# PSUM banks named by the kernel, and two kinds of loads issued by GpSimd

## The chip, the cores and the metric

The program runs on one core of one Trainium2 chip. A core has TensorE (PE; PEld is its weight load), VectorE (DVE), ScalarE (ACT) and GpSimd (POOL), and SyncE (SP), whose work here is to issue DMAs. TensorE writes its results to PSUM, which has eight banks of 128 partitions by 2 KB; a tile of this kernel's P() fills one bank. The metric is the device time of one execution in microseconds (us).

## The reference, cut to what matters

One layer of a diffusion backbone, float32, width 1024, 512 latent tokens and 256 context tokens:

1. h = modulated layer norm of the tokens; z = h @ w_in.
2. Branch A, RWKV-7 in 16 heads of 64 and both directions: each of k, r, v is a part of z with a three-tap shift along the tokens. A decay d and a gate a come from two small products after tanh. Per token, S = S diag(d) - (S kk)(kk a)^T + v k^T, and y = S r. The scan runs over the context first and then over the latent tokens.
3. Branch B, spatial gating; both branches are gated and projected, and added to x with a layer norm.
4. A mixture of 16 experts that choose their tokens (router, top-k, three products per expert), and the last layer norm.

## The kernel before, in words

The work falls into stages. From 0 to 305 us a loop over `ct` (eight blocks of 128 channels) makes k, r and v by zmm(), which takes one PSUM tile `zl` for the latent tokens and one `zc` for the context. shift_in() then makes the three taps: a ScalarE copy (L352) and two VectorE steps (L354, L356) that read the PSUM tiles; `kt`, `rt` and `vt` name the results for k, r and v. prep_a() multiplies the small products (PSUM tiles `b1` and `b2`, shown as `b` in the profile), prep_tanh() reads them on ScalarE (L427, L428), z_sq() follows (L402), then prep_scan() (L436 to L445, with `Ge` at L443). prep_v() transposes v (PSUM tiles `vT`, read by ScalarE at L514). One round of the loop issues, in this order: z_k(ct, 0), prep_d1(ct - 1), z_k(ct, 1), prep_v(ct - 1), prep_bonus(ct - 1), prep_a(ct, 0), prep_tanh, z_sq, prep_scan, prep_kd, z_r, prep_k, more VectorE steps, z_v, prep_a(ct, 1), prep_tanh. The loop stands in a manual schedule: each engine runs its instructions in this written order.

From 305 to 575 us TensorE makes the gating parts of z. From 575 to 862 us the scan runs, in 12 steps of 64 tokens (four of context, eight latent) and two directions. Its order is written out in a list of short words, PLAN and PLAN_END. In a word such as `s3.1` the letter is the part, then come the step and the direction: z (zed), q (query), y (you), s (state), w (why) are the products that follow one another; K is keys_t (the transposes `bk` of `xx`, L856); l loads `al` and `xx` (prep_load, with GpSimd's memsets of `al`), a makes the pairwise products (PSUM tile `sc`, VectorE L695); v loads `Dt` and starts a wave, 31 small VectorE steps (L717, L719), run by the words p; F and D end a wave; o writes to `Asd`, from which `Dt` is read (L723), i reads `x` from Xpd and `tp` from Xsd. S, U and R are loads: sv_load, uv_load and ro_load. uv_load fills one half of a tile, and in you() ScalarE writes the other half (L877, L878); state() reads both (PSUM tile `sp`, added to `sv` by VectorE, L894). Inside PLAN each engine keeps the written order; in PLAN_END and elsewhere outside a manual schedule SP, TensorE and ScalarE do, and a planner orders VectorE and GpSimd.

From 862 to 1024 us come the readout, the branches, the output projection and the router; then to the end the experts, for which 376 MB of weights and more are streamed in.

All PSUM tiles come from P(), L70. Before, it names one tag for all of them, with eight buffers: the bank of a new tile is the one that the planner's own times say is freed first. On the chip a new tile's first write waits until every reader of that bank's last tile is done.

Of the kernel before, what the change touches and what calls it, by code (L numbers as in the profile page):

```python
# [1 line left out]

# [5 lines left out]
F32 = mybir.dt.float32  # L8
# [35 lines left out]
def block_kernel(es: ExitStack, tc, x, ctx, cT, ada_w, ada_b, pc, rows, w_ch, w_vs, w2, a2, g2, sgu_w,  # L44
                 wba, wbb, w_out, rw, e1, e3, e2, out):
    nc = tc.nc
    V, S, G, PE, SY = nc.vector, nc.scalar, nc.gpsimd, nc.tensor, nc.sync
# [6 lines left out]
    pp = es.enter_context(tc.tile_pool(name="ps", bufs=8, space=PSUM))  # L54
# [5 lines left out]
    def nm(p):  # L60
        cnt[0] += 1
        return f"{p}{cnt[0]}"

    def T(shape, name="t", dt=F32):
        return big.tile(shape, dt, name=nm(name), tag="big", bufs=NBIG)

    def K(shape, name="t", dt=F32):
        return keep.tile(shape, dt, name=nm(name), tag="keep", bufs=NKEEP)

    def P(name="p"):  # L70
        return pp.tile([128, 512], F32, name=nm(name), tag="ps")

    def mm(o, l, r, start=True, stop=True):
        PE.matmul(o, l, r, start=start, stop=stop, skip_group_check=True)  # L74
# [144 lines left out]
    def ada_chunk(ws):  # L219
        p = P("ada")  # L220
        for k in range(KT):
            g = k % 4
            mm(p[32 * g:32 * g + 32, :], sP[:, k, :], ws[k // 2][:, k % 2, :], start=(k < 4), stop=(k >= 4))
        a = T([128, 512], "adao")
        S.activation(a, p, AF.Copy)
        return a
# [9 lines left out]
    def ada_cols(n):  # L236
        a = ada_chunk(aw.pop(n))
        p = P("adt")
        for b in range(4):
            PE.transpose(p[:, b * 128:b * 128 + 128], a[:, b * 128:b * 128 + 128], ident)  # L240
        which, b0 = divmod(n * 4, 8)
        dst = md[:, which, b0:b0 + 4, :]
        V.tensor_reduce(dst, p.rearrange("p (b g m) -> p b m g", b=4, g=4)[:, :, 0:2, :], AX.X, OP.add)
        V.tensor_tensor(dst, dst, adab_col[:, which, b0:b0 + 4, None].to_broadcast([128, 4, 2]), OP.add)
        if which == 1:
            V.tensor_scalar(dst, dst, 1.0, None, op0=OP.add)
# [23 lines left out]
    for d in range(2):  # L270
        for lst, src, nme in ((w2p, w2, "w2p"), (a2p, a2, "a2p")):
            t = T([128, D], nme)
# [7 lines left out]
    def hl(k):  # L280
        return hL[0][k // 2][:, k % 2, :], hL[1][k // 2][:, k % 2, :]

    def hc(k):
        return hC[0][k // 4][:, k % 4, :], hC[1][k // 4][:, k % 4, :]
# [23 lines left out]
    for k in range(KT):  # L308
        if k % 4 == 0:
            ada_cols(k // 4)  # L310
            ada_cols(k // 4 + 2)
            if k:
                zw.step()
        for (dst, i0, n, j) in ((hl(k), 2, 4, 0), (hc(k), 0, 2, 1)):
            p = P("ht")
            w = n * 128
            for i in range(n):
                PE.transpose(p[:, i * 128:i * 128 + 128], xts[i0 + i][:, k * 128:k * 128 + 128], ident)
            t = T([128, TL], "hf")
            V.tensor_scalar(t[:, :w], p[:, :w], md[:, 1, k, j:j + 1], md[:, 0, k, j:j + 1], op0=OP.mult, op1=OP.add)  # L320
            S.activation(dst[0], t[:, :w], AF.Copy)
            G.tensor_tensor(dst[1], t[:, :w], dst[0].bitcast(F32), OP.subtract)  # L322

    def zmm(w, want_ctx):
        wh, wl = (t.rearrange("p (k n) -> p k n", k=KT) for t in w)
        pl = P("zl")
        pc_ = P("zc") if want_ctx else None
        for k in range(KT):
            st, sp = k == 0, k == KT - 1
            hh, hlo = hl(k)  # L330
            mm(pl, wh[:, k, :], hh, st, False)
            mm(pl, wh[:, k, :], hlo, False, False)
            if want_ctx:
                ch_, cl = hc(k)
                mm(pc_[:, :TC], wh[:, k, :], ch_, st, False)
                mm(pc_[:, :TC], wh[:, k, :], cl, False, False)
                mm(pc_[:, :TC], wl[:, k, :], ch_, False, sp)
            mm(pl, wl[:, k, :], hh, False, sp)
        return pl, pc_
# [31 lines left out]
    Rd_ = dp.tile([2, KT, 128, NCL, C], F32, name="Rhd")  # L371
# [262 lines left out]
    def cidx(si, d):  # L634
        lat, s = steps[si]
        n = NCL if lat else NCX
        return lat, (n - 1 - s if d else s)
# [10 lines left out]
    AL, XX, AP_, TP, X1, BK, RO, UV, SV = {}, {}, {}, {}, {}, {}, {}, {}, {}  # L648
# [7 lines left out]
    def halves(e):  # L656
        return (slice(0, 64), slice(64, 128)) if e == 0 else (slice(64, 128), slice(0, 64))
# [161 lines left out]
                r0 = e * 64  # L819
                S.activation(tp[r0:r0 + 32, d, :, 32:64], pv[r0:r0 + 32], AF.Copy)  # L820

    def vload(dst, si, d):
        lat, c = cidx(si, d)
        t0 = (TC if lat else 0) + (c ^ d) * C
        src = Vd[d][t0:t0 + C, :].rearrange("t (c e n) -> t c e n", c=KT, e=2)
        SY.dma_start(dst[64:128, 0], src[:, :, 0, :])
        SY.dma_start(dst[0:64, 1], src[:, :, 1, :])

    def sv_load(si):
        for d in range(2):  # L830
            SV[si, d] = T([128, 2, KT, C], "sv")
            vload(SV[si, d], si, d)

    def uv_load(si):
        for d in range(2):
            lat, c = cidx(si, d)
            UV[si, d] = T([128, 2, KT, C], "uv")
            vload(UV[si, d], si, d)

    def ro_load(si):  # L840
        for d in range(2):
            lat, c = cidx(si, d)
            if lat:
                ro = RO[si, d] = st_tp["ro", d, si % 2]
                for e in range(2):
                    own, oth = halves(e)
                    SY.dma_start(ro[own, e], Rd_[d, :, own, c, :].rearrange("c p n -> p c n"))

    def keys_t(si):
        for d in range(2):  # L850
# [29 lines left out]
    def state(si, d):  # L880
        bk, sv, uv, svn = BK.pop((si, d)), SV[si, d], UV[si, d], SV[si + 1, d]
        u = uidx(si, d)
        sp = P("sp").rearrange("p (c n) -> p c n", c=KT)
        idt = (si, d) in IDENT
        if idt:
# [115 lines left out]
    def finish(_):  # L1001
# [31 lines left out]
        ('b', 3): ((wave, 1),),  # L1033
        ('a', 4): ((static_pair, 0), (xx_load, 1),),
        ('a', 6): ((sv_load, 0), (uv_load, 0), (wave_in, 0), (wave_in, 1),),
        ('a', 3): ((xx_load, 0),),
    }
# [45 lines left out]
    for d in range(2):  # L1083
# [16 lines left out]
        "q10.1 p1 s9.1 U11 s9.0 w9 V10 h10.0 z10.1 X10 z10.0 p1 y10.1 h10.1 y10.0 p5 s10.1 R11 s10.0 p4 w10 p2 "  # L1100
        "i11 p1 z11.0 h10.2 p1 V11 p1 q11.1 X11 z11.1 h11.0 y11.0 q11.0 p3 y11.1 p2 h11.1 w11 h11.2 "
    ).split()
    IDENT = {(1, 0), (4, 0), (4, 1), (7, 1), (8, 0), (8, 1), (9, 1), (10, 1)}

    def finish_wave(w):
# [9 lines left out]
    def run_plan(plan, hook=None):  # L1115
        for t in plan:
            args = [int(a) for a in t[1:].split(".") if a]
            if t[0] == "h":
                hook(*args)
            elif t[0] == "t":  # L1120
                static_pair(1)
            else:
                OPS[t[0]](*args)
# [40 lines left out]
    def readout(half):  # L1164
        H = [K([128, 4, 256], "yAH", F32R) for _ in range(2)]
        L = [K([128, 4, 256], "yAL", F32R) for _ in range(2)]
        YA[half] = (H, L)
        for o, i in enumerate(HALF[half]):
            bo = GB[half][0][o]
            for b in range(2):  # L1170
                p = P("yT").rearrange("p (a n) -> p a n", a=4)
                pg = P("gg").rearrange("p (a n) -> p a n", a=4)
                t = T([128, 4, 128], "yf")
                for q in range(4):
                    ct = 4 * b + q
                    PE.transpose(p[:, q, :], yt[i][:, ct * 128:ct * 128 + 128], ident)
                    mm(pg[:, q, :], st_tp["g2"][:, ct * 128:ct * 128 + 128], sdg[:, i * 128:i * 128 + 128])
                for q in range(4):
                    ct = 4 * b + q
                    if b == 0:  # L1180
                        V.scalar_tensor_tensor(t[:, q, :], p[:, q, :], col("lnx_g", ct), bo[:, ct, :], op0=OP.mult, op1=OP.add)
                    else:
                        S.activation(t[:, q, :], p[:, q, :], AF.Copy, scale=col("lnx_g", ct))
                if b:
                    G.tensor_tensor(t, t, bo[:, 4 * b:4 * b + 4, :], OP.add)
                V.tensor_mul(t, t, pg)
                hd, ld = H[b][:, :, o * 128:o * 128 + 128], L[b][:, :, o * 128:o * 128 + 128]
                S.activation(hd, t, AF.Copy)
                V.tensor_tensor(ld, t, hd.bitcast(F32), OP.subtract)
# [169 lines left out]
    def early(si, at):  # L1359
# [8 lines left out]
        if si == nst - 1:  # L1368
# [4 lines left out]
            if at == 1:  # L1373
                readout(0)

    with tc.manual_schedule():
        run_plan(PLAN)
    run_plan(PLAN_END, early)
# [25 lines left out]
    ps = out_mm(0, (0, 1), MG.pop(0))  # L1404
# [7 lines left out]
    ps = out_mm(1, (0,), mg)  # L1412
    sid1 = out_ln(1, (0,), ps)
    next(sid1), next(sid1)
    ps = out_mm(1, (1,), mg, True)
# [28 lines left out]
    for r in range(8):  # L1444
        src = wk if r else affT
# [6 lines left out]
    p = P("sT")  # L1452
# [132 lines left out]
    e, hidT = NE - 1, hidTs.pop(NE - 1)  # L1585
# [100 lines left out]
```

## Time and profile before

| | us |
|---|---|
| runs of the kernel before | 1973.10, 1976.82, 1978.05 |
| median | 1976.82 |
| profiled execution | 1979.77 |
| its span | 1978.0 |
| TensorE busy | 1762.2 |
| VectorE busy | 919.3 |
| ScalarE busy | 604.2 |
| GpSimd busy | 239.2 |

How to read it: the profile is of one execution. A busy share over the whole span says little here, as the stages differ; the rows below give the stages apart. In a row of waits, "PE b L74 <- ACT vs L514" reads: TensorE's instruction on tile `b`, line 74, stood idle until ScalarE's instruction on `vs`, line 514, was done. A line can be that of a helper: all matmuls stand on L74, so the tile's name tells them apart. All DMAs are issued by SP; the page lists 48 of `uv<-Vd` and 32 of `ro<-Rhd`, 128 KB each.

### The profile page before, as it was taken

The numbers are of one execution on the slowest core, as the hardware profiler recorded it, in microseconds if no ns is written. First come the engines' busy times: TensorE is split into PE (matmuls) and PEld (weight loads), VectorE is DVE, ScalarE is ACT, GpSimd is POOL, SyncE is SP. The second block draws the span as 40 slices with busy tenths as digits, with TensorE's granted clock in tenths as the row PEclk, the third lists the DMA queues.
The fourth block names the chain that finished last, engine by engine and source line by source line (L and its number), as shares of the span: only waits on it lengthen the run. The fifth ranks groups of instructions, "written<-read, shape, count | busy, mean of one in ns | idle before, by whom it ended". The sixth has DMA issues, their size and how long they took to land.

```text
span 1978.0 us, 32483 instructions
## 1 busy us (share of the span) xinstructions
PE 1762.2 (89%) x13252; PEld 1122.8 (57%) x13252; DVE 919.3 (46%) x1685; ACT 604.2 (31%) x1058; POOL 239.2 (12%) x203
## 2 busy tenths in 40 slices
PE   6989999999987978788959999899998989899895
PEld 3877777878876867687844434334343323334324
DVE  6688886687837768786950020110102002020105
ACT  2666766233246645343221111101011101111101
POOL 4422234110110100055300000000000000000000
PEclk9999999999999989898969999999999999999998
DMA  9265657667697667584189999999999999999995
GB/s 331 92 194 155 188 155 238 193 225 228 237 261 160 154 146 179 114 266 138 65 348 427 426 428 426 426 427 427 426 427 427 427 427 426 427 427 427 427 418 201
DMA packets 363757, 590.34 MB, mean 298 GB/s; under 512 B 220372, under 2 KB 282324, under 8 KB 315480
## 3 DMA queue, kind: packets, MB, share of 16 engines
q1 hardware_dynamic: 363608, 588.26, 80.6%
q8 instruction: 105, 1.72, 0.3%
q14 instruction: 44, 0.36, 0.1%
HBM read 539.69 MB, written 47.71 MB: 297 GB/s over the span
## 4 chain that ended last, share of the span: by engine, by line
DMA 44%; PE 26%; DVE 11%; issue 3%; SPq 2%; ACT 1%; POOL 0%; DVEq 0%; ACTq 0%; POOLq 0%
DMA we<-in_e 42%; PE zl L74 5%; PE hh L74 3%; PE zv L74 2%; PE sc L74 2%; DVE tmpi L717 2%; PE bb L74 2%; DVE Xt L719 2%; PE yx L74 2%; PE qs L74 2%; PE yp L74 1%; PE sp L74 1%; PE zp L74 1%; PE l L74 1%; PE up L74 1%
## 5 line engine op out<-in xcount | busy, mean ns | idle before, releaser
L74 PE MATMUL hh<-we,xe 128*64 128x512 f32 x2048 | 463.1, 597 | 24.5 <-DMA we<-in_e 24.2
L74 PEld LDWEIGHTS hh<-we,xe 128*64 128x64 f32 x2048 | 148.9, 137 | 324.6 <-issue 267.1
L74 PE MATMUL ye<-we,hidT 128*64 128x512 f32 (+1 forms) x1216 | 254.7, 533 | 37.8 <-DMA we<-in_e 37.5
L1521 DVE TENSOR_TENSOR hd<-hd,hh 64x512 f32<-64x512 f32 x64 | 44.1, 690 | 519.1 <-ACT hd L1520 518.7
L74 PE MATMUL zl<-hL,H 128*128 128x512 f32 x816 | 259.6, 400 | 1.9 <-DVE hf L320 1.2
L74 PEld LDWEIGHTS ye<-we,hidT 128*64 128x64 f32 x1216 | 83.3, 136 | 201.3 <-DMA we<-in_e 106.0
L1520 ACT ACTIVATE hd<-hh 64x512 f32<-64x512 f32 x64 | 37.9, 592 | 491.6 <-PE hh L74 491.6
L74 PEld LDWEIGHTS zl<-hL,H 128*128 128x128 f32 x816 | 153.9, 191 | 30.6 <-issue 2.6
L160 POOL TENSOR_TENSOR L<-w,H 128x1024 fp32r<-128x1024 f32 x54 | 138.4, 2571 | 236.6 <-ACT H L159 197.5
L74 PE MATMUL zl<-hL,L 128*128 128x512 f32 x408 | 162.1, 397 | 2.5 <-DVE L L160 2.5
L1614 POOL TENSOR_TENSOR x<-x,row 128x1024 f32<-128x1024 f32 x2 | 4.6, 2340 | 989.3 <-DVE rv L129 989.3
L159 ACT ACTIVATE H<-w 128x1024 fp32r<-128x1024 f32 x91 | 95.0, 1054 | 88.5 <-DMA w<-in_w_ch 36.1
L1539 ACT ACTIVATE ye<-ye 64x512 f32<-64x512 f32 (+1 forms) x34 | 18.9, 555 | 272.8 <-PE ye L74 272.5
L1540 DVE SCALAR_TENSOR_TENSOR ye<-ye,gate,srow 64x512 f32<-64x512 f32 (+1 forms) x38 | 23.9, 663 | 149.1 <-ACT ye L1539 148.8
L74 PEld LDWEIGHTS zl<-hL,L 128*128 128x128 f32 x408 | 78.1, 191 | 14.4 <-DVE L L160 3.6
L717 DVE TENSOR_TENSOR tmpi<-Dt,Xt 128x31 f32<-128x31 f32 (+15 forms) x186 | 63.6, 342 | 18.0 <-DMA Dt<-Asd 12.5
L719 DVE TENSOR_TENSOR Xt<-Xt,tmpi 128x31 f32<-128x31 f32 (+15 forms) x186 | 63.8, 343 | 6.4
L74 PEld LDWEIGHTS xe<-oh,h 128*128 128x128 f32 x512 | 59.6, 196 | 8.9 <-issue 8.9
L74 PE MATMUL co<-ye,ohT 128*128 128x512 f32 (+1 forms) x144 | 62.7, 591 | 0.0
L74 PE MATMUL xe<-oh,h 128*128 128x128 f32 x512 | 61.8, 282 | 0.7 <-DVE oh L1470 0.7
L74 PEld LDWEIGHTS zc<-hC,H 128*128 128x128 f32 x288 | 54.0, 188 | 12.7 <-POOL hC L322 0.4
L1496 DVE COPY gate<-gate 64x1 f32<-64x1 f32 x16 | 2.5, 156 | 122.7 <-PE gate L74 122.4
(332 smaller groups left out, 2908.8 us busy)
## 6 DMA issues: line engine op xcount, KB each, us to landing
we<-in_e SPq DMA_DIRECT2D x376, 1024.0 KB, 19.6
w<-in_w_ch SPq DMA_DIRECT2D x51, 512.0 KB, 5.0
w<-in_ada_w SPq DMA_DIRECT2D x32, 512.0 KB, 5.6
xx<-Xkd SPq DMA_DIRECT2D x28, 512.0 KB, 5.6
adaw<-in_ada_w SPq DMA_DIRECT2D x16, 512.0 KB, 10.3
we<-in_e SPq DMA_DIRECT2D x32, 256.0 KB, 5.4
Xkd<-g SPq DMA_DIRECT2D x32, 192.0 KB, 2.7
Ald<-al SPq DMA_DIRECT2D x16, 384.0 KB, 2.3
```

The source lines that it names most:

```text
L74: PE.matmul(o, l, r, start=start, stop=stop, skip_group_check=True)
L159: S.activation(h, t, AF.Copy)
L160: (eng or G).tensor_tensor(l, t, h.bitcast(F32), OP.subtract)
L717: V.tensor_tensor(tv, Dt[:, j, None, j + 1:].to_broadcast([128, m, n]), X[:, 0:m, j:j + 1].to_broadcast([128, m, n]), OP.mult)
L719: V.tensor_tensor(X[:, 0:m, j + 1:], X[:, 0:m, j + 1:], tv, OP.subtract)
L1496: V.tensor_copy(g[j * 64:j * 64 + 64], p[j * 64:j * 64 + 64, j:j + 1])
L1520: S.activation(hd, pn[n][0:64], AF.Silu)
L1521: V.tensor_tensor(hd, hd, pn[n][64:128], OP.mult)
L1539: S.activation(y, p, AF.Copy)
L1540: V.scalar_tensor_tensor(y, p if same else y, gv[e - j][rs], gt2[rs, cs], op0=OP.mult, op1=OP.mult)
L1614: G.tensor_tensor(acc[i], acc[i], l2[0], OP.mult)
```

## The change

It has two parts. P() gives each tile a bank of its own name, ps0 to ps7, with one buffer each. As long as the list `order` holds something, the bank is its next digit; it is filled with the 258 digits of BANKS just before PLAN runs. Otherwise it is the next bank in turn whose last tile nobody in the program text still holds (counted by Python's references); where all are held, simply the next. `del p, t` drops two such references. And vload() takes the queue as an argument: uv_load() gives it GpSimd, ro_load() issues on GpSimd too, and sv_load() stays on SP.

```diff
+    banks, nextb, order = {}, [0], []
+
     def P(name="p"):
-        return pp.tile([128, 512], F32, name=nm(name), tag="ps")
+        if order:
+            b = order.pop(0)
+        else:
+            b = next((x % 8 for x in range(nextb[0], nextb[0] + 8)
+                      if x % 8 not in banks or sys.getrefcount(banks[x % 8]) <= 2), nextb[0] % 8)
+            nextb[0] = b + 1
+        banks.pop(b, None)
+        banks[b] = t = pp.tile([128, 512], F32, name=nm(name), tag=f"ps{b}", bufs=1)
+        return t
...
+    del p, t
...
-    def vload(dst, si, d):
+    def vload(dst, si, d, q=SY):
...
-        SY.dma_start(dst[64:128, 0], src[:, :, 0, :])
-        SY.dma_start(dst[0:64, 1], src[:, :, 1, :])
+        q.dma_start(dst[64:128, 0], src[:, :, 0, :])
+        q.dma_start(dst[0:64, 1], src[:, :, 1, :])
...
-            vload(UV[si, d], si, d)
+            vload(UV[si, d], si, d, G)
...
-                    SY.dma_start(ro[own, e], Rd_[d, :, own, c, :].rearrange("c p n -> p c n"))
+                    G.dma_start(ro[own, e], Rd_[d, :, own, c, :].rearrange("c p n -> p c n"))
...
+    BANKS = (
+        "0123456701234567012345670123456701235647012356041235670412356704123670415243672041536720415376240153"
...
+    order += [int(b) for b in BANKS]
     with tc.manual_schedule():
         run_plan(PLAN)
     run_plan(PLAN_END, early)
```

## Rows read from the trace of the kernel before

**Rows 1.** Busy time of each engine (instructions), TensorE clock, DMA share, GB/s, by stage.
```profile
0.00:305.00 305.00, 265.31 (x1401) 211.95 (x1402) 246.51 (x322) 192.47 (x297) 97.00 (x82) 0.98 0.60 189
305.00:575.00 270.00, 265.85 (x1269) 218.66 (x1267) 193.91 (x324) 98.15 (x149) 41.44 (x41) 1.00 0.72 229
575.00:862.00 287.00, 229.98 (x5403) 212.34 (x5404) 207.17 (x485) 151.39 (x319) 36.28 (x50) 0.94 0.72 168
1024.00:1978.00 954.00, 869.86 (x4273) 361.09 (x4272) 141.37 (x263) 106.50 (x204) 4.64 (x2) 0.98 0.99 415
```

**Rows 2.** TensorE's waits, 0 to 305 us: total us, times, longest.
```profile
PE b L74 <- ACT vs L514: 19.0, 7, 3.3
```

**Rows 3.** The same, 575 to 862 us.
```profile
PE bk L856 <- DVE qs L907: 10.8, 1, 10.8
PE yp L74 <- DVE sv L894: 10.4, 1, 10.4
PE bk L856 <- DVE sv L894: 9.0, 1, 9.0
...
PE bk L856 <- DVE al L695: 4.5, 5, 1.9
```

**Rows 4.** Timeline of VectorE, ct = 1: start us, us, instruction, [idle before].
```profile
110.90 0.75 DVE L356 SCALAR_TENSOR_TENSOR kt<-zl,pcol,kt 128x511 f32<-128x511 f32 x1
...
117.99 0.75 DVE L354 SCALAR_TENSOR_TENSOR rt<-zl,pcol,rt 128x511 f32<-128x511 f32 x1 [2.64 <-ACT rt L352]
```

**Rows 5.** Timeline of TensorE, ct = 1.
```profile
101.99 0.80 PE L74 MATMUL b<-xp,wp 128*128 128x512 f32 x1
...
106.36 0.50 PE L74 MATMUL b<-xc,wp 128*128 128x256 f32 x2 [3.34 <-ACT vs L514]
...
114.53 1.02 PE L74 MATMUL b<-sq,bones 128*128 128x512 f32 x2
```

**Rows 6.** VectorE's waits, 0 to 305 us.
```profile
DVE sq L502 <- ACT sq L498: 6.6, 7, 0.9
```

**Rows 7.** Timeline of ScalarE, ct = 1.
```profile
107.20 0.72 ACT L427 ACTIVATE g<-b,pcol 128x512 f32<-128x512 f32 x1
...
108.70 0.53 ACT L428 ACTIVATE a<-b,pcol 128x256 f32<-128x256 f32 x1
111.74 0.94 ACT L402 ACTIVATE sq<-kt,pcol 128x768 f32<-128x768 f32 x1 [2.51 <-DVE kt L356]
...
114.60 0.85 ACT L443 ACTIVATE Ge<-L 128x768 f32<-128x768 f32 x1 [0.99 <-DVE L L438]
```

**Rows 8.** VectorE's waits: 641 to 664, 705 to 720, 817 to 829 us.
```profile
DVE sv L894 <- PE sp L74: 4.3, 2, 4.0
DVE qs L907 <- PE qs L74: 3.7, 2, 2.3
...
DVE al L695 <- ACT ap L692: 6.8, 1, 6.8
...
DVE qs L907 <- PE qs L74: 5.1, 1, 5.1
```

**Rows 9.** Timeline of SP's queue, around wave 2.
```profile
602.60 0.63 SPq L827 DMA_DIRECT2D uv<-Vd  x1
603.41 0.49 SPq L723 DMA_DIRECT2D Dt<-Asd  x1
```

**Rows 10.** Timeline of VectorE, start of wave 2.
```profile
609.47 0.19 DVE L717 TENSOR_TENSOR tmpi<-Dt,Xt 128x31 f32<-128x31 f32 x1 [3.11 <-DMA Dt<-Asd]
```

**Rows 11.** Timeline of VectorE, one line in two rounds.
```profile
88.98 0.95 DVE L473 TENSOR_TENSOR g<-L,kd 128x768 f32<-128x768 f32 x1
...
105.17 3.13 DVE L473 TENSOR_TENSOR g<-L,kd 128x768 f32<-128x768 f32 x1
```

**Rows 12.** DMA issues, 575 to 862 us: KB each, median us to landing.
```profile
uv<-Vd SPq DMA_DIRECT2D x44, 128.0 KB, 4.1
```

**Rows 13.** Timeline of ScalarE, after the U1 loads.
```profile
606.50 0.59 ACT L877 ACTIVATE uv<-up 64x512 f32<-64x512 f32 x1 [0.28 <-PE up L74]
```

More of the change, by code (lines that the diff above doesn't have):

```diff
@@ L1 @@
+import sys
 from contextlib import ExitStack
@@ L1102, in block_kernel @@
     ).split()
+    BANKS = (
+        "0123456701234567012345670123456701235647012356041235670412356704123670415243672041536720415376240153"
+        "7624015376240153762401624501632745016327415603274156302756413027564132064715320647153210536247103562"
+        "4710356245671034256714256714250367142560731425607314256073"
+    )
     IDENT = {(1, 0), (4, 0), (4, 1), (7, 1), (8, 0), (8, 1), (9, 1), (10, 1)}
```

## The prediction

> **What bounds the kernel now.** I read the table by stage first [rows 1]. The last 954 us stream expert weights with the DMA engines 0.99 busy; that stretch starts when the work before it ends, so any time won or lost before 1024 us goes through to the end one for one. Before it lie three stages that the change can touch. In the first 305 us TensorE is busy 265 us and VectorE 247 us. From 305 to 575 us TensorE is busy 265.85 of 270 us: it has no slack there, and hands on whatever shift it arrives with. From 575 to 862 us, the scan, TensorE is busy 230 and VectorE 207 of 287 us: neither is full, they wait for each other.
>
> Then the waits of TensorE. In the first stage one row stands out, `b` after ScalarE's copies of `vT`: 19.0 us in 7 waits [rows 2]. `b` reads weights and `xp`, `xl`, `xc`, none of which comes from those copies; so it waits for a PSUM bank that `vT` held. In the scan four rows are of the same kind [rows 3]: `bk` is a transpose of `xx` by a constant and reads nothing of VectorE's, yet it waits 10.8, 9.0 and 4.5 us for VectorE. The `yp` wait of 10.4 us ends the same way, with VectorE's last read of an older `sp`. That is 34.7 us of TensorE waiting for banks that were handed out badly, and the change hands them out anew. What it is worth is read from VectorE, whose chain runs on through these places.
>
> **The change part by part.** The sum is made against the profiled execution, 1979.8 us (span 1978.0 us, 1.8 us around it); the median of the runs shown is 1976.8 us, 3.0 us lower, and I carry the difference over to it.
>
> *Rotation in the first stage: a loss.* Outside the written list the new P() takes the next bank in turn that nobody holds. In a round of the loop over `ct` the calls come in the order zl, zc (of z_k), vT four times, bon, b2, b1, b1, zl (of r), two of prep_k, zl, zc (of v), b2, b1, b1. The first `b1` of prep_a(ct, 0) is the eighth call after the `zl` of z_k: it gets that bank, and the second gets that of `zc`. Those tiles are let go in Python by then (z_k's second part pops them), but on the chip VectorE reads them last in the two `kt` steps. For ct = 1 the second of these ends at 111.65 us [rows 4], whereas TensorE wants to start `b` at 101.99 us, and did [rows 5]. Before, it waited once, until 106.36 us; now the first `b1` can't start before 111.65.
>
> What that does to the loop: its period is set by VectorE's chain, which waits once for ScalarE, 2.64 us before `rt` at 117.99 us [rows 4], and otherwise only 0.9 us [rows 6]. So the question is when `rt` can start after `kt`. Before: 117.99 - 111.65 = 6.3 us. After, on ScalarE: the four tanh, 107.20 to 109.23 us [rows 7], lay ahead of the `kt` end; now they lie behind it, since they read `b`. The first `b1` takes 1.03 us (106.36 - 3.34 - 101.99 [rows 5]), so tanh runs from 112.7 to about 115.1 us, and `sq`, at 111.74 before, starts 3.4 us later. ScalarE waited 0.99 us for VectorE before `Ge` [rows 7]; VectorE's scan is later as well, but a wait of that size mostly goes. So `rt` comes at 117.99 + 3.4 - 0.9 = about 120.5 us, **+2.5 us** per round. On TensorE the rest (four more matmuls of `b`, zl of r) took 106.36 to 114.53 = 8.2 us, much of it at the lower of the two clock levels (1.2 GHz) after the wait; 111.65 + 1.03 + 8.2 + 0.7 for ScalarE's copy gives 121.6 us, +3.6: the upper end, if each of the longer waits drops the clock. The lower end is 1.5, if VectorE gets back what it loses to GpSimd (below). Seven rounds (ct = 1 to 7): 7 x 2.5 = **+17.5 us**, ends +10 and +25. From 305 us on the rotation has no such pair: readers are done long before the eighth call. The full TensorE then carries the shift to 575 us.
>
> *The written list in the scan: a gain.* By the times of before I put each of the 258 digits on its tile: nearly every new holder starts over 1.5 us after the last reader of the old one. So the waits of rows 3 go, and what follows them moves up until the next thing is late. At 640 us: TensorE does the transposes, `sp` and the two `sc` in the 9.0 us in which VectorE finishes its wave, and VectorE's idle time right behind, 4.3 + 3.7 us [rows 8], falls by 7.4; then Dt, which starts from these results, is late next and moves along. At 705 us: VectorE's 6.8 us; `sc` still waits about 0.3 us for a bank: 6.5. At 818 us: 5.1 us. The 4.5 us of the last row of rows 3 lie beside a VectorE that hardly rests in that stretch: 0 to 1.2, 1 taken. Sum **-20 us**; the ends are -12 (VectorE's written order keeps half) and -30 (TensorE's whole waits).
>
> *Loads moved from SP to GpSimd.* 48 + 32 DMAs of 128 KB leave SP's queue at 0.63 us each, as at 602.60 us [rows 9]: some 50 us of a queue that hardly rests in the scan. What waited behind them: Dt of wave 2, issued at 603.41 us behind four of these loads, and VectorE then idle 3.11 us for it [rows 9, 10]; four times 0.63, about 2.4 us of it, goes. At the scan's start the loads of `x` from Xpd stand behind four as well (four times 0.63 us; 1.5 taken), and two later waves' Dt behind some (1). Sum **-5 us**, ends 0 and -8.
>
> GpSimd is busy 36.3 of 287 us in the scan [rows 1], so there is room, but the trace has no DMA issued by it; I bound the price by SP's 0.63 us below and by the 3.1 us that GpSimd's or VectorE's slowest contended instruction took above [rows 11]. At 1 us, 80 DMAs are 80 us and fit. They queue in written order with its memsets: a load waits behind a memset that waits for a buffer, and the other way round. The place with no slack is U1: its loads landed 4 to 5 us after issue (4.1 us [rows 12]), and ScalarE writes the other half of the tile from 606.50 us [rows 13], just then. Four DMAs at 1.1 us instead of 0.63 are +2 us there: **+2 us** taken, nearer SP's price as GpSimd is idle; 0 and +10 at the ends (4 x 2.5).
>
> The Trainium skill speaks against this half. "SBUF — State Buffer", section "SBUF: two separate sides", says that GpSimd writes the descriptors of its own DMAs, and can't while VectorE holds the port pair that they share; it gives 3100 ns for a DMA of 620 ns. No DMA of GpSimd's is in this trace; that the two engines hold each other up is: the same product takes 0.95 us, and 3.13 us in another round, beside a GpSimd split [rows 11].
>
> After 862 us rotation returns, over tiles that are read soon after they are written: 0, ends -2 and +3.
>
> **Sum:** +17.5 - 20 - 5 + 2 = -5.5 us; 1979.8 - 5.5 = 1974.3, and 3 lower on the median: about **1971.5 us**.
>
> **Rivals.** (a) *The stall in the first stage is larger than the gain.* Each wait for `kt` is 4 to 10 us long, TensorE comes back at the lower clock (after the wait of 3.34 us, `b` and zl ran slow), and a round costs 3.6 us: +25, with -15 in the scan and +2: +12, 1988.8 us. It decides once a round costs over 3.3 us. For: the granted clock of this stage is 0.98 with such waits [rows 1], so it does dip; against: ScalarE's chain, not TensorE's, is the longer one at full clock.
> (b) *GpSimd issues late.* At 3.1 us a DMA, U1 is 10 us late and the memsets behind U2 and R4 hold up two preps, 5 us each at least beyond what the waits of before hide: +20 in place of +2 and of SP's -5 only half kept: +15, 1992 us. It decides from about 2 us a DMA. Against: most U and R loads have 10 us and more of slack.
> (c) *The rotation doesn't stall*, because the bank is passed over as still held: -23 us, 1953.8. For: P() asks for holders; against: the tile is popped a call earlier.
> (d) *No change*: the gain of the scan is eaten by VectorE's written order (12 instead of 20) : +2 us, 1978.
>
> **How the numbers follow.** Forecast 0.42, (a) 0.16, (b) 0.13, (c) 0.14, (d) 0.15. The forecast's own range is 1962 to 1982 (the first stage's term off by 7, the scan's by 8: 10 either way). For 8 in 10 I reach from 1954 to 1990. A measurement of this kernel tells about 0.3%, 5.9 us, from no change: faster means below 1970.9. The forecast lies half beyond that bound (0.21, and 0.16 inside, 0.05 above), (c) is faster, (d) is mostly same (0.11; 0.02 faster, 0.02 slower), (a) and (b) are mostly slower (0.24), with 0.03 same and 0.02 faster: faster 0.39, same 0.30, slower 0.31.
>
> **What would show it.** Right: `b` waits in the first stage for VectorE's `kt`, 7 times, 4 to 10 us each, and the second stage starts 15 to 25 us later; `bk` and `yp` no longer wait for VectorE in the scan, and it is about 25 us shorter. Wrong: no longer waits of `b` (then (c)); PE waits for `uv` or `al` loads, or VectorE's wait for Dt grows (then (b)).

## The result, and the profile after

The changed kernel takes 1989.34 us (median of 5 runs, 1988.87 to 1994.90) against 1976.82 us (1972.25 to 1978.93): ratio 1.0076, 95% interval 1.0055 to 1.0097. It is slower by some 0.8%, where a small gain was forecast; the span of its profiled execution is 1987.2 us against 1978.0.

The same stretches of the changed kernel (columns as in [rows 1]); its lines lie 11 to 19 further down in the code:

```profile
0.00:305.00 305.00, 255.22 (x1311) 204.79 (x1312) 227.44 (x306) 179.58 (x274) 86.90 (x77) 0.94 0.56 177
305.00:575.00 270.00, 261.65 (x1253) 216.93 (x1252) 198.18 (x326) 102.42 (x157) 46.35 (x44) 0.98 0.67 216
575.00:862.00 287.00, 250.55 (x5355) 228.00 (x5355) 218.44 (x494) 154.18 (x321) 90.41 (x131) 0.96 0.76 188
1024.00:1978.00 954.00, 870.20 (x4276) 361.44 (x4276) 145.36 (x277) 107.91 (x206) 4.64 (x2) 0.98 0.99 413
```

The fixed stretches already show the shift: in the first 305 us TensorE now does 10 us less work, VectorE 19 us less. GpSimd's busy time in the scan grew by 54 us, which is 80 DMAs of 0.68 us. Where the time went is seen better by following the same instructions through both traces (start times, us):

| instruction | before | after | shift |
|---|---|---|---|
| last round's `rt` (VectorE) | 310.3 | 332.1 | +21.7 |
| first `vg` copy (ScalarE) | 329.7 | 352.8 | +23.1 |
| first `bk` copy, the scan begins (ScalarE) | 573.8 | 599.9 | +26.1 |
| wave 2 begins (VectorE) | 609.5 | 633.1 | +23.6 |
| wave 3 begins | 676.2 | 692.4 | +16.3 |
| wave 4 begins | 739.1 | 749.9 | +10.8 |
| copy that ends wave 5 | 815.9 | 827.6 | +11.7 |
| last `sv` add | 845.1 | 853.5 | +8.4 |
| last `y` add | 873.4 | 881.4 | +8.0 |
| first `hh` matmul, the experts (TensorE) | 1028.5 | 1038.5 | +10.1 |
| last `ye` matmul (TensorE) | 1953.0 | 1961.7 | +8.7 |

So the first stage lost 23 us and 3 more up to the scan; the scan gave back 18 us of the 26; behind it 2 us were lost again. The loss of the first stage shows in one row, the waits of TensorE in that stage (to 330 us, since the seventh ends after 305 us now), in place of [rows 2]:

```profile
PE b L85 <- DVE kt L369: 37.1, 7, 9.2
```

One round of it, ct = 1, on VectorE ([rows 4]), TensorE ([rows 5]) and ScalarE ([rows 7]), and TensorE from 110 to 114 us (busy, granted clock, DMA share, GB/s):

```profile
110.20 0.75 DVE L369 SCALAR_TENSOR_TENSOR kt<-zl,pcol,kt 128x511 f32<-128x511 f32 x1
...
114.54 0.56 DVE L449 TENSOR_SCALAR g<-g 128x768 f32<-128x768 f32 x1 [2.99 <-ACT g L441]
...
120.70 0.75 DVE L367 SCALAR_TENSOR_TENSOR rt<-zl,pcol,rt 128x511 f32<-128x511 f32 x1 [2.51 <-ACT rt L365]
```

```profile
111.10 0.76 PE L85 MATMUL b<-xp,wp 128*128 128x512 f32 x1 [9.21 <-DVE kt L369]
...
113.37 0.63 PE L85 MATMUL b<-xc,wp 128*128 128x256 f32 x2
```

```profile
110.00:114.00 4.00, 2.90 (x9) 0.50 1.14 302
```

```profile
112.33 0.69 ACT L440 ACTIVATE g<-b,pcol 128x512 f32<-128x512 f32 x1 [5.65 <-PE b L85]
114.03 0.48 ACT L441 ACTIVATE g<-b,pcol 128x256 f32<-128x256 f32 x1 [1.02 <-PE b L85]
...
115.33 0.94 ACT L415 ACTIVATE sq<-kt,pcol 128x768 f32<-128x768 f32 x1
...
117.08 0.85 ACT L456 ACTIVATE Ge<-L 128x768 f32<-128x768 f32 x1
...
119.97 0.69 ACT L365 ACTIVATE rt<-zl,pcol 128x512 f32<-128x512 f32 x1
```

The last `kt` step ends at 110.95 us and `b` starts 0.15 us later, after 9.21 us of waiting. TensorE comes back at half of its clock, the lower level of 1.2 GHz (0.50 granted), and its six groups for `b` take from 111.10 to 113.8 us. ScalarE's tanh waits for them (1.02 us even between two of its own), `sq` starts at 115.33 instead of 111.74, VectorE waits 2.99 us for `g`, and `rt` starts 9.75 us after `kt`, where it was 6.3. In the scan the three long waits of [rows 3] are gone. The fourth row is nearly as it was, 3.9 us where it was 4.5; these are the two largest of TensorE's waits for VectorE that are left:

```profile
PE zp L85 <- DVE sv L908: 5.9, 5, 3.5
PE bk L869 <- DVE al L708: 3.9, 3, 2.6
```

### The profile page after: what moved, and what is told of

The parts are those of the page before. It is cut to its first block, busy times and chain, and to the rows that moved or that the text cites. A ratio compares the mean times of both kernels' runs of the same rounds, so it can differ in the third digit from the quotient of the medians.

```text
span 1987.2 us, 32519 instructions
## 1 busy us (share of the span) xinstructions
PE 1773.1 (89%) x13252; PEld 1133.2 (57%) x13252; DVE 919.8 (46%) x1685; ACT 604.3 (30%) x1058; POOL 289.9 (15%) x283
## 2 busy tenths in 40 slices
DMA packets 325359, 590.35 MB, mean 297 GB/s; under 512 B 179413, under 2 KB 241365, under 8 KB 277081
## 3 DMA queue, kind: packets, MB, share of 16 engines
q0 software_dynamic: 3840, 10.49, 2.0%
## 4 chain that ended last, share of the span: by engine, by line
DMA 36%; PE 13%; DVE 5%; issue 1%; POOL 0%; SPq 0%; ACT 0%; DVEq 0%; POOLq 0%
DMA we<-in_e 36%; PE hh L85 6%; PE ye L85 2%; PE yx L85 2%; PE co L85 1%; PE xe L85 1%; PE lg L85 0%; PE ba L85 0%; PE hT L1550 0%; DVE mt L1232 0%; DVE x L1290 0%; DVE mgL L1236 0%; DVE wk L1466 0%; DVE m L1465 0%; PE h2T L1336 0%
## 5 line engine op out<-in xcount | busy, mean ns | idle before, releaser
L85 PE MATMUL hh<-we,xe 128*64 128x512 f32 x2048 | 463.5, 597 | 23.6 <-DMA we<-in_e 23.3
L171 POOL TENSOR_TENSOR L<-w,H 128x1024 fp32r<-128x1024 f32 x54 | 133.7, 2485 | 274.5 <-ACT H L170 255.3
L85 PEld LDWEIGHTS zl<-hL,L 128*128 128x128 f32 x408 | 78.5, 192 | 14.5 <-DVE L L171 3.4
```

What stands on the lines that cost most here:

```text
L171: (eng or G).tensor_tensor(l, t, h.bitcast(F32), OP.subtract)
```

## The experiments

The experiments recombine four things: what names the banks ahead of the scan, in it and behind it (before's numbers, the list, or in turn), and who issues the loads. e6, e8 and e9 add something of their own. Ratios are to runs of the kernel before on the same chip.

| kernel | banks ahead / in / behind the scan | loads | median us | ratio, interval |
|---|---|---|---|---|
| after | turn / list / turn | GpSimd | 1989.3 | 1.0076, 1.0055 to 1.0097 |
| e1 | as before / list / turn | GpSimd | 1961.1 | 0.9928, 0.9900 to 0.9956 |
| e2 | as before in all | GpSimd | 1972.6 | 0.9974, 0.9948 to 1.0000 |
| e3 | turn / list / turn | SP | 1990.9 | 1.0077, 1.0048 to 1.0107 |
| e4 | as before / list / as before | GpSimd | 1959.1 | 0.9904, 0.9869 to 0.9940 |
| e5 | as before / list / as before | SP | 1963.5 | 0.9917, 0.9890 to 0.9944 |
| e6 | after, TensorE kept at work | GpSimd | 1978.2 | 1.0014, 0.9995 to 1.0034 |
| e7 | as before / turn / turn | GpSimd | 1970.1 | 0.9964, 0.9940 to 0.9988 |
| e8 | e4, two splits moved | GpSimd | 1950.5 | 0.9881, 0.9859 to 0.9904 |
| e9 | e8, one split moved further | GpSimd | 1938.7 | 0.9828, 0.9783 to 0.9873 |

**e1: the first stage's banks as before.** The digits are those that the kernel before gave its first 247 tiles.

```diff
+    FIRST = (
+        "0716234507162345071623450716234750612457036215403175402675314207631057632457106235410375412675034217"
...
-    banks, nextb, order = {}, [0], []
+    banks, nextb, order = {}, [0], [int(b) for b in FIRST]
```

> The changed kernel, with one edit: the 247 PSUM tiles ahead of the scan get the bank numbers that they had in the kernel before, instead of plain rotation; scan list and GpSimd loads stay. Theory (the rotation holds b1 behind kt, 26 us by the two traces at 575 us): b waits 19 us for the vT copies again, not 37 for kt; the scan starts near 575 us, and the time is 1989.3 - 26 = about 1963 us, some 0.7% under the kernel before. Rival 1 (the loss sits in GpSimd's loads): about 1985 us or more. Rival 2 (the scan gains only because it starts late, with its weights and loads already there): the scan gives back most of the shift, 1975 to 1980 us.

Measured 1961.1 us, as the theory said; Rival 2 falls as well, since here the scan starts 0.4 us earlier than in the kernel before and still gains 18.2 us. `b` waits for the copies of `vT` again:

```profile
PE b L90 <- ACT vs L532: 19.7, 7, 3.3
```

The whole loss, and more than the changed kernel's 0.8%, is the rotation ahead of the scan: 1.0076 against 0.9928 is 1.5%, some 28 us (1989.3 to 1961.1) by one digit string.

**e2: the loads alone; e3: the banks alone.** In e2 the kernel before gets the four lines of the change that turn SY to q or G; in e3 they are turned back:

```diff
-            vload(UV[si, d], si, d, G)
+            vload(UV[si, d], si, d)
...
-                    G.dma_start(ro[own, e], Rd_[d, :, own, c, :].rearrange("c p n -> p c n"))
+                    SY.dma_start(ro[own, e], Rd_[d, :, own, c, :].rearrange("c p n -> p c n"))
```

> The kernel before with only the uv and ro loads issued by GpSimd; PSUM tiles as before. Theory (GpSimd issues at 0.68 us a DMA, nearly SP's price, and SP is relieved): 1972 to 1977 us, the first 305 us unchanged. Rival (GpSimd's issue is what made the changed kernel slower): 1985 us or more, with TensorE or ScalarE waiting for uv.

> The changed kernel with the uv and ro loads back on SP: banks by rotation and list alone. Theory (the loads' move is worth about 2 us of the scan's gain, and the list was drawn up for an order of events with the loads on GpSimd): 1990 to 1995 us, first stage as in the changed kernel. Rival (GpSimd's loads cost time): 1980 us or less.

Both came out on the theory's side, 1972.6 and 1990.9 us: GpSimd's issuing costs nothing that the total shows. Rival (b) of the prediction falls. Whether moving the loads gains anything is at the edge of e2's interval (up to 1.0000).

**e4: behind the scan as before too.** As e1, with the 284 digits of before appended to BANKS.

```diff
-    order += [int(b) for b in BANKS]
+    order += [int(b) for b in BANKS + LAST]
```

> As e1, and the 284 PSUM tiles behind the scan get the bank numbers of the kernel before as well, so that the list and the loads are all that is left of the change. Theory (the shift grows by 3 us between 900 and 950 us in the changed kernel because rotation returns there): 3 us less than e1, about 1960 us. Rival (that growth comes from the planner's order of VectorE and GpSimd, not from banks): as e1 within 1 us.

2.0 us under e1 by the medians, which the intervals don't tell apart. The traces don't settle it either: from the last `sv` add to the first `hh` matmul e1 loses 2.9 us against the kernel before (-19.8 to -16.9) and e4 0.2 us (-38.6 to -38.3), as the theory has it; but e5, which has the numbers of before there too, loses 3.7 us, and e7, which has rotation there, 0.9 us. What rotation costs behind the scan stays open.

**e5: the list alone.** As e4 with e3's edit.

> As e4 (bank numbers of before ahead of the scan and behind it, the written list in it), with the uv and ro loads back on SP: the list is all that is left of the change. Theory (the loads' move is worth 3 to 6 us, as in e2 against the kernel before): 1962 to 1965 us, 13 to 15 us under the kernel before. Rival (with the list in place TensorE and VectorE bind, and SP's queue no longer matters): as e4 within 1.5 us.

1963.5 us lies in the theory's span; the intervals of e4 and e5 overlap, so what the loads are worth beside the list stays open in the totals. The traces, from the scan's first `bk` copy to the last `y` add against the kernel before, one execution each, say how much shorter it is: list and loads 18.1 us (after), 18.2 (e1) and 19.8 (e4), list alone 14.5 (e3) and 10.6 (e5), loads alone 5.2 (e2), rotation and loads 11.1 (e7). So the list gives 11 to 15 us and the loads 4 to 9 (e3 against after, e5 against e4).

**e6: TensorE kept at work before `b1`.** The changed kernel, with matmuls whose sums nobody reads:

```diff
         p2 = P("b2")
+        if d == 0 and ct:
+            for _ in range(16):
+                mm(p2, w2p[d][:, cs], dwt[d][0][0], True, True)
```

> The changed kernel with 16 extra matmuls into the b2 tile ahead of the first b1 in rounds 1 to 7 (their sums are overwritten), so that TensorE doesn't stand idle while b1 waits for kt. Theory (a round costs 3.2 us and not the 2.5 forecast because b runs at the lower clock after the wait, at 0.50 of the full one from 110 to 114 us): b and zl run at full clock, a round gets about 1 us shorter, 1982 us. Rival (ScalarE's and VectorE's chain behind b sets the round whatever the clock): 1988 to 1990 us.

1978.2 us, 11 us less, although TensorE does 4.2 us more per round. A later round in the changed kernel (`b` starts at 216.33 us), and the same in e6:

```profile
216.33 0.47 PE L85 MATMUL b<-xp,wp 128*128 128x512 f32 x1 [4.31 <-DVE kt L369]
```

```profile
215.00:219.00 4.00, 2.67 (x10) 0.78 1.15 300
```

```profile
208.19 4.21 PE L85 MATMUL b<-xp,wp 128*128 128x512 f32 x16
213.18 0.47 PE L85 MATMUL b<-xp,wp 128*128 128x512 f32 x1 [0.78 <-DVE kt L369]
```

```profile
211.00:215.00 4.00, 3.22 (x17) 1.00 1.06 269
```

```profile
PE b L85 <- DVE kt L369: 12.0, 7, 5.6
```

In this round the wait before `b` shrinks from 4.3 to 0.8 us, the clock from 211 to 215 us is 1.00 where it was 0.78 from 215 to 219, and the last round's `rt` comes 12.5 us later than before the change instead of 21.7. From the first round to the last 22.4 us are lost in the changed kernel and 12.1 in e6, on average 3.2 and 1.7 us a round.

The first of these rounds, ct = 1, tells whether it is the clock or the added matmuls as such. There they end 5.6 us before `b` can start, and the clock has fallen again (TensorE, e6):

```profile
112.13 0.76 PE L85 MATMUL b<-xp,wp 128*128 128x512 f32 x1 [5.56 <-DVE kt L369]
```

```profile
110.00:114.00 4.00, 1.87 (x6) 0.50 1.07 271
```

This round lost 3.3 us in e6 and 3.4 in the changed kernel: with the clock at 0.50 in both, the matmuls gained nothing. In the five rounds behind it, in which `b` starts within 0.8 us of them, e6 lost 1.0 to 1.3 us a round and the changed kernel 2.5 to 3.8 (in the last round 3.3 and 5.1).

**e7: rotation in the scan.** e1 without the line that fills `order` from BANKS.

> As e1 (first stage with the bank numbers of before), without the written list: the scan's tiles get banks by plain rotation. By the times of before, rotation leaves 7 short conflicts of together 7 us on TensorE in the scan, most of them where VectorE is the later engine. Theory (any even turn over the eight banks takes the three waits of 9 to 11 us away; the list's own order is worth little): 1961 to 1965 us. Rival (it is the list's order that wins the scan): 1972 us or more.

1970.1 us lies between the two: neither was right. Two of the long waits are back, in other places than the times of before had shown (TensorE's waits, 560 to 850 us):

```profile
PE bk L874 <- DVE qs L925: 9.4, 1, 9.4
...
PE bk L874 <- DVE sv L912: 4.7, 1, 4.7
```

Laid over the times of before, rotation had 7 us of conflicts; but each wait, and each wait that is gone, moves the times that the next one depends on. Against e1 the list's own order, beyond an even turn, is worth some 7 us of the scan (18.2 against 11.1).

**e8 and e9: the first stage's other loss.** e2's and e4's traces had something that the trace of before hadn't: partway through the first stage its rounds became shorter. VectorE's `g` and `L` products of e2:

```profile
156.69 3.17 DVE L488 SCALAR_TENSOR_TENSOR L<-L,a 128x768 f32<-128x768 f32 x1
...
167.64 3.12 DVE L473 TENSOR_TENSOR g<-L,kd 128x768 f32<-128x768 f32 x1
...
188.72 0.95 DVE L488 SCALAR_TENSOR_TENSOR L<-L,a 128x768 f32<-128x768 f32 x1
...
197.46 0.95 DVE L473 TENSOR_TENSOR g<-L,kd 128x768 f32<-128x768 f32 x1
```

In rounds with 3.1 us products the round takes 32.1 us, later 28.8. The long ones stand beside a GpSimd split that began just before. e8 moves two of the splits behind the steps that they preceded, e9 one of them further:

```diff
-            zw.step()
             z_k(ct, 1)
             if ct:
                 prep_v(ct - 1)
                 prep_bonus(ct - 1)
                 flush()
+            zw.step()
...
             z_v(ct)
+            prep_a(ct, 1)
+            prep_tanh(ct, 1)
             zw.step()
             if ct > KT - 3:
                 zw.step()
-            prep_a(ct, 1)
-            prep_tanh(ct, 1)
```

(This is e9's; in e8 the first zw.step() stands right behind z_k(ct, 1).)

> As e4, with two of the weight splits (ScalarE copy, GpSimd subtract) moved behind the steps that they preceded in each round of the first stage. In e2's and e4's traces the rounds in which VectorE's g and L products take 0.95 us are 28.8 us long, and those in which one or both take 3.1 us beside a GpSimd split are 32.1 us long. Theory (the split that starts just before such a product holds VectorE up, and the order of the split decides it): the products take 0.95 us in most rounds, the scan starts 15 to 20 us earlier, 1940 to 1945 us. Rival (the collision only moves on to other products): 1955 to 1962 us.

> As e8, with the first of the two moved splits one step further back, behind ScalarE's copies of vT. In e8's trace VectorE's L product of direction 1 still takes 3.03 us in every round, because the split starts 0.3 us before it; TensorE waits 10.1 us in 7 times for the vT copies, which stand behind the split's ScalarE half. Theory (the later of two colliding instructions waits for the earlier, so only the order of starts counts): both products take 0.95 us, a round is 29.9 - 2.1 = 27.8 us unless TensorE binds first at about 28.8, so 7 to 14 us less than e8, 1937 to 1944 us. Rival (TensorE already binds in e8's rounds): 1948 to 1951 us.

e8: 1950.5 us, between theory and rival: one product is short now, the other isn't. The split began 0.26 us ahead of it and ended at 134.38 us; the product ended 0.82 us after that, about the time that it takes alone (VectorE, then GpSimd, e8):

```profile
132.17 3.03 DVE L506 SCALAR_TENSOR_TENSOR L<-L,a 128x768 f32<-128x768 f32 x1
```

```profile
131.91 2.47 POOL L176 TENSOR_TENSOR L<-w,H 128x1024 fp32r<-128x1024 f32 x1 [6.11 <-ACT H L175]
```

e9: 1938.7 us, as the theory said; both products are short in every round, and TensorE hardly waits for the copies of `vT` (e8's row, then e9's two products and row):

```profile
PE b L90 <- ACT vs L532: 10.1, 7, 3.2
```

```profile
129.41 0.95 DVE L491 TENSOR_TENSOR g<-L,kd 128x768 f32<-128x768 f32 x1
130.40 0.96 DVE L506 SCALAR_TENSOR_TENSOR L<-L,a 128x768 f32<-128x768 f32 x1
```

```profile
PE b L90 <- ACT vs L532: 2.2, 2, 1.6
```

A round takes 28.5 us, 1.4 less than in e8 (29.9), although the product alone is 2.1 us shorter. How much of it comes from the product and how much from the shorter wait for `vT`, both of which the one edit changed, is not separated. e9 beats both kernels: 1.7% under the kernel before, and 2.5% under the changed one (1938.7 / 1989.3, medians that were not run side by side).

## Why the prediction was wrong

**The step that failed** is the price of a round of the first stage, "+2.5 us per round", and with it "+17.5 us". The mechanism was as written: `b1` takes the bank of `zl` and waits for VectorE's last `kt` step, seven times, 4 to 9 us each (37.1 us). But a round cost 3.2 us (22.4 us over seven rounds, from -0.7 to +21.7), and with what follows in the stage and up to the scan it came to +26.1. I had put the clock at the upper end, because at full clock ScalarE's chain is the longer one. From the end of `kt` to `rt` the prediction has 6.3 + 2.5 = 8.8 us; measured are 9.75 in the round shown, and, in the later round of e6's rows, 9.6 in the changed kernel and 8.25 in e6 (VectorE; the changed kernel, then e6):

```profile
215.44 0.75 DVE L369 SCALAR_TENSOR_TENSOR kt<-zl,pcol,kt 128x511 f32<-128x511 f32 x1
...
225.78 0.75 DVE L367 SCALAR_TENSOR_TENSOR rt<-zl,pcol,rt 128x511 f32<-128x511 f32 x1 [3.16 <-ACT rt L365]
```

```profile
212.29 0.75 DVE L369 SCALAR_TENSOR_TENSOR kt<-zl,pcol,kt 128x511 f32<-128x511 f32 x1
...
221.29 0.75 DVE L367 SCALAR_TENSOR_TENSOR rt<-zl,pcol,rt 128x511 f32<-128x511 f32 x1 [2.29 <-ACT rt L365]
```

So at full clock the price would have been enough (1.9 us over the 6.3), and the clock added 1.3 to 1.5 us. The lower clock slowed `b` itself, the first link of ScalarE's chain, and not only the `zl` matmuls beside it: that is where the argument broke. In the round shown `sq` was to start 3.5 us behind the end of `kt` and started 4.4 us behind it, and that is the whole of this round's miss. In the later round TensorE's chain is the longer one as well, by 0.75 us (ScalarE, the changed kernel):

```profile
225.06 0.69 ACT L365 ACTIVATE rt<-zl,pcol 128x512 f32<-128x512 f32 x1 [0.75 <-PE zl L85]
```

VectorE's wait for `g`, 2.99 us in the round shown, stands beside the chain: ScalarE no longer waits before `Ge`, as forecast. Four of the seven rounds did lose just 2.5 us, but that is luck, for VectorE got some 0.8 us of each back: one of its two slow products beside GpSimd became short (3.16 to 0.95 us), while another instruction, `g` at L449, grew from 0.55 to 1.99 us. The working also has a slip: it lets the four tanh end at about 115.1 us, where 2.03 us [rows 7] behind 112.7 is 114.7.

**The list in the scan**, "-20 us", gave 11 to 15. Its single places came out nearly as priced: at 640 us 7.3 us (7.4 forecast: wave 3 from +23.6 to +16.3), at 705 us 5.5 (6.5); with the list alone (e3) 6.0 and 5.8. From there to wave 5 nothing more came (1 forecast). At 818 us the wait went, 5.1 forecast, but only 3.3 are left at the last `sv` add. There the planner orders VectorE, and it put five small steps, 848.13 to 851.38 us, between `gv` and `sv`, which followed each other before (first the kernel before, then the changed one). Two of them took 0.97 and 1.82 us, where the next takes 0.18, beside a GpSimd product:

```profile
841.86 1.22 DVE L1142 TENSOR_REDUCE gv<-gsq 128x16 f32<-128x1024 f32 x1 [0.63 <-POOL gsq L1140]
843.00 1.38 DVE L895 TENSOR_TENSOR sv<-sp,gC 64x512 f32<-64x512 f32 x2
```

```profile
848.13 0.97 DVE L140 TENSOR_SCALAR rv<-gv 128x32 f32<-128x32 f32 x1
849.14 1.82 DVE L141 TENSOR_SCALAR rt<-rv 128x32 int32<-128x32 int32 x1
850.99 0.18 DVE L142 TENSOR_SCALAR ry<-rt 128x32 int32<-128x32 int32 x1
...
851.38 1.39 DVE L908 TENSOR_TENSOR sv<-sp,gC 64x512 f32<-64x512 f32 x2
```

```profile
847.17 3.75 POOL L1170 TENSOR_TENSOR bo<-bo,pcol 128x1024 f32<-128x1024 f32 x2 [0.33 <-POOL gsq L1158]
```

**The loads**, "-5" and "+2", were right in sign: 4 to 9 us gained by the traces, where 3 were forecast. Up to wave 2 the changed kernel gained 2.4 us (+26.1 to +23.6), the size put on Dt of wave 2, where the list alone (e3) lost 0.6. GpSimd's price is 0.68 us a DMA, next to SP's 0.63 [rows 9], not the 1.1 that I took. These are the DMA rows of the changed kernel and a row of GpSimd:

```profile
uv<-Vd POOLq DMA_DIRECT2D x48, 128.0 KB, 3.5
...
ro<-Rhd POOLq DMA_DIRECT2D x32, 128.0 KB, 5.3
```

```profile
625.54 0.68 POOL L840 DMA_DIRECT2D uv<-Vd  x1
```

The prediction left out which VectorE instructions hold the port pair. The Trainium skill ("SBUF — State Buffer", section "SBUF: two separate sides") has GpSimd locked out while VectorE runs an instruction that takes both ports, such as an fp32 copy in SBUF, and infers that a two-input product does not keep it from writing descriptors. The trace agrees on both: beside the waves' two-input products the DMAs took 0.68 us, and the only two of the 80 above 0.85 us, 1.22 and 1.17 us, began while VectorE copied `Dt` and ended 0.28 us after that copy (the first of them, GpSimd, then VectorE):

```profile
718.66 1.22 POOL L839 DMA_DIRECT2D uv<-Vd  x1
```

```profile
718.56 1.04 DVE L751 COPY Dt<-Xt 64x1024 f32<-64x1024 f32 x1
```

The same section's rule that a VectorE instruction with two SBUF inputs and a GpSimd one that reads SBUF exclude each other is what e8 and e9 show: 3.03 to 3.17 us against 0.95.

**Behind the scan**, 0 forecast, 2 us were lost up to the experts, of which 1.4 were back at the last `ye` matmul.

**The sum.** Against the profiled execution of before, the changed kernel's took 9.2 us more (1989.02 - 1979.77), where -5.5 was forecast. Of these 14.7 us the first stage makes 8.6 (26.1 for 17.5) and the scan 4.9 (18.1 gained for 23). The gap of the medians is 3 us wider: the prediction carried the 3.0 us by which the profiled execution of before lay above the median over to the changed kernel, whose own lies at its median.

**The choice among the rivals.** Rival (a) named what happened, with 3.6 us a round, 15 in the scan and 1988.8 us; measured 1989.3. That its time is met to 0.5 us is luck: a round cost 3.2 us, the 25 us were reached by what came after the rounds, the scan gave 18.1 us where (a) has 13, and the 3 us of the medians made up for it. It was given 0.16, since the forecast leaned on the case at full clock, while the trace of before already had the granted clock at 0.70 after a wait of 3.34 us (before, 106 to 110 us):

```profile
106.00:110.00 4.00, 3.64 (x13) 0.70 0.33 122
```

## What to carry to other kernels

Turning over the PSUM banks in order couples a tile to the one eight calls earlier; check the longest-lived tile of a loop against that distance, and name the banks there by hand. When a wait of some microseconds (4.3 and more here) comes before TensorE's work on the critical chain, look at the granted clock behind such a wait in the trace, and price the work at that clock. Where VectorE and GpSimd both run products over SBUF, look in the trace for the same instruction with two durations: moving the GpSimd ones past it was worth 15 to 20 us here (e4 to e9, by the ratios and by the medians; with the shorter wait for `vT`), about as much as list and loads together (19 us, before to e4).

## What the runs showed of the hardware that was not expected

The same loads travel in other packets when GpSimd issues them. The 80 DMAs, 10.49 MB, are 3840 packets on its queue (2.7 KB each), and packets under 512 B fell from 220372 to 179413: by 40959, some 512 per DMA, which are 256 bytes each. The `uv` loads landed a little sooner (3.5 against 4.1 us), the `ro` loads later (5.3 against 3.3).

```profile
q1 hardware_dynamic: 321368, 577.77, 77.9%
q0 software_dynamic: 3840, 10.49, 2.0%
```

The first stage has two steady rhythms with the same code, 32.1 and 28.8 us a round; the kernel before stayed in the slow one throughout its profiled execution, e2 and e4 left it after some rounds. It may be why the runs of before spread over 1955.5 to 1983.6 us and those of e8 only over 1949.7 to 1954.0; no run traces that for before.
